# Holding the second-half weights of the output projection behind the first half's, in a one-layer hybrid encoder kernel on Trainium2

## The chip, the cores and the metric

The kernel runs on one core of one Trainium2 chip. A core has a matrix engine (TensorE, "PE" in the profile, with its weight loads shown as "PEld"), a vector engine (VectorE, "DVE"), a scalar engine (ScalarE, "ACT"), a general engine (GpSimd, "POOL") and a queue engine (SyncE, "SP") that mostly asks for transfers between the chip's memory and the core's on-chip memory. Each engine works through its own list of instructions strictly in order; an instruction that waits for another engine or for a transfer holds up all that stands behind it in its list. The metric is the device time of one execution in microseconds (us); the time of a kernel is the median of several executions.

## The reference, cut to what matters

One layer (DEPTH = 1) over 512 tokens of width 1024, with 16 learned tokens put in front and dropped at the end:

```
u      = rmsnorm(h, norm_mix)
proj   = u @ w_in
y_rw   = rwkv7_branch(proj[...])            # 512 columns
y_fx   = fox_branch(proj[...])              # 512 columns
merged = gate_A * (y_rw @ w_out_rw) + gate_B * (y_fx @ w_out_fx)
h      = h + merged @ w_o                   # the output projection
z      = rmsnorm(h, norm_mlp)
h      = h + square(relu(z @ w_up)) @ w_down
```

The change touches the line with `w_o`, a product of 512 x 1024 by 1024 x 1024.

## The kernel before

**Products in three passes.** Every large matrix product is done with operands split in two: a "hi" part, which is the float32 value copied to the matrix engine's shorter float format, and a "lo" part, which is what the copy left out. The product is hi x hi + hi x lo + lo x hi (`passes`, L276), so each tile of weights costs three matmuls, and before that one copy on ACT and one subtraction on DVE. Weights come in chunks of 128 x 512 float32 (256 KB): one transfer on SP's queue into a "raw" tile, then the ACT copy to hi, then the DVE subtraction to lo.

**Two ways of loading a chunk.** `load_h` (L232) takes raw, hi and lo from rings of four tiles each, called wraw, whi and wlo; `load_w` (L242) calls it for two chunks. A new load has to wait until the raw tile of the chunk four before has been read by its subtraction, and a new hi has to wait until the matrix engine has finished with the chunk four before. The list `asked` collects the transfers asked for by `load_h`; it is used later on to order other transfers behind them. `split` (L272) does only the copy and the subtraction (L273 and L274), into whatever tiles it is given.

**The stage around the change.** The work ahead of it merges the two branches: for each of eight column blocks m, two gate tiles gl come in by transfer (L1207), ACT takes their tanh (L1208), the matrix engine makes two products into accumulation banks po (L1213), DVE multiplies each bank by its gate (L1215, which frees the bank), GpSimd adds the two (L1217), ACT writes the hi part mhi (L1218) and DVE the lo part mlo (L1219). After the last mhi one table load on ACT (`pinned`, L265) prepares for later functions. The banks po come from a ring of four.

Then comes the output projection, in two halves of 512 output columns:

- First half (L1236 to L1244): the eight chunks of `wo[0]` come through `load_w`, so through the rings of four. They are called chunk 0 to chunk 7 here. The matrix engine goes through them in this order: for chunks 0 to 5, all four row blocks with one chunk (12 matmuls) before the next chunk; chunks 6 and 7 are taken together, row block by row block. The four sums pd are two po banks and two others; the second po bank is the one that held the second product of merge block m = 6.
- Second half (L1245 to L1248): the eight chunks of `wo[1]` have a place of their own. Their raw tiles are slices of one large tile, shown as zhiraw, which is free at this time, and their hi and lo parts are slices of wohi and wolo. Nothing in a ring holds these loads and splits back.
- After that the first-half sums are added to h (L1254 to L1257), the matrix engine runs the second half (L1274) row block by row block with the transposes (L1264) of the normalised rows between them, and the up-projection follows (L1302), whose first chunks were loaded early (L1234, into zloraw), and whose further chunks come through `load_w` again.

**What sets the order.** In this part of the program nothing fixes the order of the lists by hand. The compile step lays out each engine's list from its own model of times, preferring what is traced first among what it takes to be ready; so a step that is traced later, but is ready sooner in that model, can be placed ahead of an earlier one. The helper `after(ins, prev)` (L251) adds an edge that only orders: `ins` is placed behind `prev`, with no semaphore.

Of the kernel before, what the change touches and what calls it, by code (L numbers as in the profile page):

```python
# [9 lines left out]
F32 = mybir.dt.float32  # L10
# [4 lines left out]
ALU = mybir.AluOpType  # L15
# [172 lines left out]
def kernel(ctx, tc, ht, x, win, par, cst, gain, lora, wout, wo, wup, wdn, out, dbg=None):  # L188
    nc = tc.nc
# [3 lines left out]
    V, G, A = nc.vector, nc.gpsimd, nc.scalar  # L193
# [35 lines left out]

    asked = []  # L230

    def load_h(src, low, tag, bufs):  # L232

        raw = wp.tile([128, 512], F32, name=tag + "raw", bufs=bufs[0])
        asked.append(nc.sync.dma_start(raw, src))
        hi = wp.tile([128, 512], F32R, name=tag + "hi", bufs=bufs[1])
        lo = wp.tile([128, 512], F32R, name=tag + "lo", bufs=bufs[2])
        A.copy(hi, raw)  # L238
        low.tensor_tensor(lo, raw, hi.bitcast(F32), ALU.subtract)  # L239
        return hi, lo  # L240

    def load_w(src, low=(V, V)):  # L242

        return [load_h(src[:, 512 * j:512 * j + 512], low[j], "w", (4, 4, 4)) for j in range(2)]
# [5 lines left out]
    def after(ins, prev):  # L250

        tc.add_manual_dep(ins.ins, prev.ins.name, mybir.DependencyInfo(mybir.DependencyClass.NoSync, mybir.DependencyReason.DATA),
                          reason="one accumulation at a time")
# [16 lines left out]
        return table["pin"]  # L270

    def split(hi, lo, x):  # L272
        A.copy(hi, x)  # L273
        V.tensor_tensor(lo, x, hi.bitcast(F32), ALU.subtract)  # L274

    def passes(w, x):  # L276
        return ((w[0], x[0]), (w[0], x[1]), (w[1], x[0]))
# [8 lines left out]
    with ExitStack() as st:  # L286
# [40 lines left out]
        with tc.tile_pool(name="xp", bufs=2) as xp:  # L327
# [7 lines left out]
            for blk in (B_LORA, B_GD, B_PAIR + 3):  # L335
# [3 lines left out]
                for j in range(2):  # L339
                    raw = wp.tile([128, 512], F32, name="wraw", bufs=4)  # L340
# [57 lines left out]
            with tc.manual_schedule(engines={ET.PE, ET.Activation, ET.DVE, ET.Pool}):  # L398
# [79 lines left out]
                shifts[1](pos[1][1], tks[1])  # L478
            tanh(lf[:64], lf[:64])
            split(lhi[:, B_LORA, :], llo[:, B_LORA, :], lf)  # L480
        y_rw = yp.tile([128, 4, S], F32, name="y_rw")
        y_fx = yp.tile([128, 4, S], F32, name="y_fx")
# [13 lines left out]
        tanh(gf, gf, scale=0.5)  # L496
        V.tensor_scalar(gf, gf, 0.5, 0.5, ALU.mult, ALU.add)
        split(lhi[:, B_GD, :], llo[:, B_GD, :], gf)

        fp = st.enter_context(tc.tile_pool(name="fp", bufs=1))  # L500
# [107 lines left out]
        def divided():  # L608
            yield chained[1]
            for k in range(2):  # L610
                split(*two(0, k), y_rw[:, k, :])
            for k in range(3):
                yield fox_done[k]
                split(*two(1, k), y_fx[:, k, :])
            yield normalised[1][1]
            for k in range(2, 4):
                split(*two(0, k), y_rw[:, k, :])
# [578 lines left out]
    with ExitStack() as st:  # L1196
# [24 lines left out]
        wohi = mp.tile([128, KB, 512], F32R, name="wohi")  # L1221
        wolo = mp.tile([128, KB, 512], F32R, name="wolo")
# [7 lines left out]
        for j in range(2):  # L1230
            we = yp.tile([128, 2, 2, 512], F32R, name=f"we{j}", tag=("y_rw", "y_fx")[j])
            for x in range(2):
                raw = raws[1][:, 2 * j + x, :]
# [5 lines left out]
        for b2 in range(4):  # L1239
            w = load_w(wo[0, b2])  # L1240
            for i, b1 in [(i, b1) for b1 in range(2) for i in range(4)] if b2 < 3 else [(i, b1) for i in range(4) for b1 in range(2)]:
                k = 2 * b2 + b1
                for n, (a, b) in enumerate(passes(M, w[b1])):
                    mm(pd[i], a[:, k, 128 * i:128 * i + 128], b, start=k == 0 and n == 0, stop=k == 7 and n == 2)  # L1244
        for k in range(KB):  # L1245
            raw = raws[0][:, k, :]
            nc.sync.dma_start(raw, wo[1, k // 2][:, 512 * (k % 2):512 * (k % 2) + 512])
            split(wohi[:, k, :], wolo[:, k, :], raw)  # L1248
        zhi = hp.tile([128, KB, S], F32R, name="zhi", tag="zhi")
        zlo = hp.tile([128, KB, S], F32R, name="zlo", tag="zlo")  # L1250
        ssb = mp.tile([128, 4], F32, name="ssb")
# [309 lines left out]
```

## Time and profile before

| | us |
|---|---|
| median of 3 runs | 840.73 (839.65 to 841.92) |
| the profiled execution's own time | 840.95 |
| its span, from first to last instruction | 839.2 |
| PE busy | 826.2 |
| DVE busy | 606.9 |
| ACT busy | 451.9 |
| merge of the branches and output projection, PE | about 395 to 509 of the span |

The granted clock of the matrix engine was 1.000. The profile is of one execution; all times in it count from the first instruction. Lines with "L1244" and the like name a line of the program; a line of a helper (L238, L239, L273, L274) stands for all who call it, so there the tile names tell who it is: whi and wlo from wraw are chunks of the rings, wohi and wolo from zhiraw are the second half. A row of the timeline gives start, duration, engine, line, operation, output and inputs, and how many like it were run together ("x2"); what stands in brackets is the idle time ahead of it and what ended it. Rows of SPq are the asking for a transfer, not the transfer.

### The profile page before, as it was taken

Reading aid. Unit: us, or ns where it says so; the run is one execution under the profiler, and the core shown is the slowest. Engines: PE = TensorE matmul, PEld = TensorE weight load, DVE = VectorE, ACT = ScalarE, POOL = GpSimd, SP = SyncE. Lnnn points to the kernel's source line nnn. Section 1 sums busy time; section 2 is a strip of 40 time slices with the busy share of each in tenths; the row PEclk is TensorE's granted clock in tenths of the full one; section 3 lists DMA queues with packets and bytes.
Section 4 is the critical chain, followed back from the end, with each engine's and each line's share of the span. In section 5 each row is a group of like instructions: output and inputs, shape, how many; then the busy total and the mean of one; then the engine's idle time right before and its main releaser. Section 6 shows DMA issues by size and latency. Waiting matters only on the chain.

```text
span 839.2 us, 15281 instructions
## 1 busy us (share of the span) xinstructions
PE 826.2 (98%) x5758; PEld 679.4 (81%) x5758; DVE 606.9 (72%) x1209; ACT 451.9 (54%) x933; POOL 117.8 (14%) x121
## 2 busy tenths in 40 slices
PE   8999999999999999999999999999999999999998
PEld 6979886686997877687887789888888888888886
DVE  6897976688779665864257644975698569867988
ACT  7767539665754276644357523565445434544452
POOL 1011000001010000000022002100650065007300
PEclk9999999999999999999999999999999999999999
DMA  7231221211112220232588403631753275336531
GB/s 235 73 91 63 65 77 43 65 53 64 54 59 91 89 65 27 76 115 91 186 281 281 140 26 101 201 102 42 255 155 101 74 229 160 90 108 209 160 102 75
DMA packets 51482, 95.88 MB, mean 114 GB/s; under 512 B 5832, under 2 KB 7240, under 8 KB 51408
## 3 DMA queue, kind: packets, MB, share of 16 engines
q1 hardware_dynamic: 47680, 86.38, 32.6%
q0 software_dynamic: 1280, 4.20, 1.7%
q10 hardware_dynamic: 2448, 4.33, 1.5%
q8 instruction: 45, 0.74, 0.4%
q14 instruction: 29, 0.24, 0.1%
HBM read 88.57 MB, written 6.31 MB: 113 GB/s over the span
## 4 chain that ended last, share of the span: by engine, by line
PE 84%; DVE 6%; ACT 4%; DMA 3%; issue 2%; POOL 1%; SPq 0%; DVEq 0%; ACTq 0%; POOLq 0%
PE pj L580 24%; PE po L1302 21%; PE po L1429 12%; PE pd L1429 5%; PE po L1274 3%; PE pw L993 2%; PE psc L738 1%; PE pj L395 1%; DMA gl<-gd 1%; PE py L786 1%; PE ppt L770 1%; PE pch L1059 1%; PE po L1244 1%; PE pd L1244 1%; DVE wlo L550 1%
## 5 line engine op out<-in xcount | busy, mean ns | idle before, releaser
L580 PE MATMUL pj<-uhi,whi 128*128 128x264 f32 (+1 forms) x480 | 164.8, 343 | 0.0
L580 PE MATMUL pj<-ulo,whi 128*128 128x264 f32 (+1 forms) x480 | 154.1, 321 | 0.0
L580 PE MATMUL pj<-uhi,wlo 128*128 128x264 f32 (+1 forms) x480 | 154.0, 321 | 0.0
L239 DVE TENSOR_TENSOR wlo<-wraw,whi 128x512 fp32r<-128x512 f32 x84 | 78.6, 947 | 40.2 <-ACT whi L238 40.0
L580 PEld LDWEIGHTS pj<-uhi,whi 128*128 128x128 f32 x480 | 90.2, 188 | 14.5 <-issue 6.1
L580 PEld LDWEIGHTS pj<-ulo,whi 128*128 128x128 f32 x480 | 90.4, 188 | 7.7 <-issue 2.4
L580 PEld LDWEIGHTS pj<-uhi,wlo 128*128 128x128 f32 x480 | 90.3, 188 | 6.9
L1302 PE MATMUL po<-zhi,whi 128*128 128x512 f32 (+1 forms) x248 | 94.8, 382 | 0.0
L1302 PE MATMUL po<-zlo,whi 128*128 128x512 f32 (+1 forms) x248 | 94.8, 382 | 0.0
L1302 PE MATMUL po<-zhi,wlo 128*128 128x512 f32 (+1 forms) x248 | 94.8, 382 | 0.0
L238 ACT CAST whi<-wraw 128x512 fp32r<-128x512 f32 x84 | 51.5, 618 | 58.7 <-PE po L1302 19.5
L549 ACT CAST whi<-wraw 128x512 fp32r<-128x512 f32 x78 | 47.6, 617 | 43.1 <-PE pj L580 40.7
L550 DVE TENSOR_TENSOR wlo<-wraw,whi 128x512 fp32r<-128x512 f32 x78 | 52.7, 685 | 21.8 <-ACT whi L549 19.2
L273 ACT CAST whi<-t 128x512 fp32r<-128x512 f32 x64 | 39.9, 624 | 44.5 <-DVE wlo L274 27.2
L1429 PE MATMUL po<-wlo,fhi 128*128 128x512 f32 (+1 forms) x164 | 63.4, 387 | 0.1
L1429 PE MATMUL po<-whi,flo 128*128 128x512 f32 (+1 forms) x164 | 62.9, 384 | 0.0
L1429 PE MATMUL po<-whi,fhi 128*128 128x512 f32 (+1 forms) x164 | 62.3, 384 | 0.0
L1351 POOL TENSOR_TENSOR t<-traw 128x512 f32<-128x512 f32 x24 | 37.1, 1561 | 173.5 <-DMA traw<-in_wdn 121.3
L274 DVE TENSOR_TENSOR wlo<-t,whi 128x512 fp32r<-128x512 f32 x64 | 43.6, 689 | 24.3 <-ACT whi L273 24.1
L1318 ACT CAST fhi<-R 128x768 fp32r<-128x768 f32 (+1 forms) x32 | 30.2, 944 | 46.1 <-DVE R L1325 25.1
L1302 PEld LDWEIGHTS po<-zlo,whi 128*128 128x128 f32 x248 | 46.6, 188 | 9.1
L1302 PEld LDWEIGHTS po<-zhi,whi 128*128 128x128 f32 x248 | 46.6, 188 | 9.0
(316 smaller groups left out, 1741.4 us busy)
## 6 DMA issues: line engine op xcount, KB each, us to landing
wraw<-in_win SPq DMA_DIRECT2D x84, 256.0 KB, 2.6
wraw<-in_wup SPq DMA_DIRECT2D x60, 256.0 KB, 3.1
wraw<-in_wdn SPq DMA_DIRECT2D x48, 256.0 KB, 2.7
traw<-in_wdn SPq DMA_DIRECT2D x48, 256.0 KB, 3.6
gd<-gt ACTq DMA_DIRECT2D x16, 256.0 KB, 2.5
wraw<-in_wout SPq DMA_DIRECT2D x16, 256.0 KB, 3.9
gl<-gd SPq DMA_DIRECT2D x16, 256.0 KB, 3.6
traw<-in_wdn POOLq DMA_DIRECT2D x16, 256.0 KB, 3.2
```

Of the source, the lines that this page charges most:

```text
L238: A.copy(hi, raw)
L239: low.tensor_tensor(lo, raw, hi.bitcast(F32), ALU.subtract)
L273: A.copy(hi, x)
L274: V.tensor_tensor(lo, x, hi.bitcast(F32), ALU.subtract)
L549: after(A.copy(hi, raw), last["ACT"])
L550: after(V.tensor_tensor(lo, raw, hi.bitcast(F32), ALU.subtract), last["DVE"])
L580: mm(po, a, b[:, k, a0:a1], start=n == 0, stop=n == 23)
L1274: mm(po, a[:, k, 128 * i:128 * i + 128], b[:, k, :], start=n == 0, stop=n == 23)
L1302: mm(po[:, t0:t1], a, b[:, k, t0:t1], start=n == 0, stop=n == 23)
L1318: A.copy(fhi[:, j, a:b], R[:, a:b])
L1351: eng.tensor_tensor(t, sums[c, pair] if c in (T1, T2) else c, d, ALU.add)
L1429: mm(x[i][:, cols], a[:, k, left, 128 * rows:128 * rows + 128], c[:, cols], start=start and k == 0 and n == 0, stop=stop and k == n_pairs ...
```

## The change

The second half's transfers get an ordering edge: each is placed in SP's list behind `asked[-3]`, which at that point of the program is the transfer of chunk 5 of the first half, the third from the end. The second half's copies and subtractions get edges too: each ACT copy is placed behind the copy of chunk 7, and each DVE subtraction behind the subtraction of chunk 7 (`casts[-1]`). To have these at hand, `load_h` now keeps its two instructions in a list `casts`, and `split` returns its two. No instruction is added, removed or resized, no tile moves, and no semaphore wait is written by hand.

```diff
+    casts = []
+
     def load_h(src, low, tag, bufs):
 
         raw = wp.tile([128, 512], F32, name=tag + "raw", bufs=bufs[0])
         asked.append(nc.sync.dma_start(raw, src))
         hi = wp.tile([128, 512], F32R, name=tag + "hi", bufs=bufs[1])
         lo = wp.tile([128, 512], F32R, name=tag + "lo", bufs=bufs[2])
-        A.copy(hi, raw)
-        low.tensor_tensor(lo, raw, hi.bitcast(F32), ALU.subtract)
+        casts.append((A.copy(hi, raw), low.tensor_tensor(lo, raw, hi.bitcast(F32), ALU.subtract)))
         return hi, lo
...
     def split(hi, lo, x):
-        A.copy(hi, x)
-        V.tensor_tensor(lo, x, hi.bitcast(F32), ALU.subtract)
+        return A.copy(hi, x), V.tensor_tensor(lo, x, hi.bitcast(F32), ALU.subtract)
...
         for k in range(KB):
             raw = raws[0][:, k, :]
-            nc.sync.dma_start(raw, wo[1, k // 2][:, 512 * (k % 2):512 * (k % 2) + 512])
-            split(wohi[:, k, :], wolo[:, k, :], raw)
+            after(nc.sync.dma_start(raw, wo[1, k // 2][:, 512 * (k % 2):512 * (k % 2) + 512]), asked[-3])
+            for x, prev in zip(split(wohi[:, k, :], wolo[:, k, :], raw), casts[-1]):
+                after(x, prev)
```

## The prediction

> **What bounds the kernel now.** I read the page first, then the matrix engine's timeline in the stage of the output projection, then the lists of ACT, DVE and SP over the same stretch, and last the chain of waits.
>
> ```profile
> span 839.2 us, 15281 instructions
> ...
> PE 826.2 (98%) x5758; PEld 679.4 (81%) x5758; DVE 606.9 (72%) x1209; ACT 451.9 (54%) x933; POOL 117.8 (14%) x121
> ...
> PE 84%; DVE 6%; ACT 4%; DMA 3%; issue 2%; POOL 1%; SPq 0%; DVEq 0%; ACTq 0%; POOLq 0%
> ```
>
> The matrix engine bounds the kernel: it is busy for 826.2 of 839.2 us, so moving transfers and splits can pay only where it stands still. Around the change it stands still twice.
>
> ```profile
> 457.03 0.39 PE L1244 MATMUL po<-whi,mhi 128*128 128x512 f32 x1
> ...
> 457.49 0.39 PE L1244 MATMUL po<-whi,mlo 128*128 128x512 f32 x1
> 458.62 0.50 PE L1244 MATMUL po<-whi,mhi 128*128 128x512 f32 x1 [0.75 <-DVE gl L1215]
> ...
> 466.01 0.39 PE L1244 MATMUL pd<-whi,mlo 128*128 128x512 f32 x1
> 466.36 0.50 PE L1244 MATMUL po<-whi,mhi 128*128 128x512 f32 x1
> 467.62 0.50 PE L1244 MATMUL po<-wlo,mhi 128*128 128x512 f32 x1 [0.76 <-DVE wlo L239]
> ...
> 481.13 0.39 PE L1274 MATMUL po<-wohi,mhi 128*128 128x512 f32 x1
> ```
>
> The first half has 96 matmuls (8 chunks, 4 row blocks, 3 passes). The chain of waits gives the pace of an undisturbed run of them:
>
> ```profile
> 481.30 10.88 PE po L1274 x48
> ```
>
> 10.88 / 48 = 0.2267 us each, so 96 take 21.76 us. From the first one (457.03) to the first of the second half (481.13) it took 24.10. Lost: 2.34 us. Stall one: after 457.49 the next was due at 457.72 and came at 458.62, 0.90 late, and that matmul was 0.11 longer. Stall two: 467.62 was due 0.45 after 466.01, so it came 1.16 late, and was again 0.11 longer. That is 2.28 of the 2.34. The 36 matmuls ahead of 466.36 are those of chunks 0 to 2, so stall two is the wait for chunk 3.
>
> **Stall one, part by part.** The engine waits for DVE to empty the bank of merge block 6 (L1215).
>
> ```profile
> 456.57 1.40 DVE L274 TENSOR_TENSOR wolo<-zhiraw,wohi 128x512 fp32r<-128x512 f32 x2 [0.20 <-ACT wohi L273]
> 457.89 0.68 DVE L1215 SCALAR_TENSOR_TENSOR gl<-gl,po 128x512 f32<-128x512 f32 x1
> ```
>
> Two second-half subtractions stand straight ahead of that multiplication; second-half work isn't wanted before 481. With both moved away, the multiplication can start 457.89 - 456.57 = 1.32 us sooner and is over by 457.25, ahead of 457.72. The stall goes, with 0.5 us to spare. (Its gate's tanh is also needed, but was done before 456: the two tanhs in the next fence are those of block 7, the last.)
>
> **Stall two.** ACT's list, and what SP had asked for:
>
> ```profile
> 455.92 1.33 ACT L273 CAST wohi<-zhiraw 128x512 fp32r<-128x512 f32 x2 [1.03 <-DMA zhiraw<-in_wo]
> 457.31 0.63 ACT L1208 ACTIVATE gl<-gl 128x512 f32<-128x512 f32 x1
> ...
> 459.45 0.63 ACT L1208 ACTIVATE gl<-gl 128x512 f32<-128x512 f32 x1 [1.00 <-DMA gl<-gd]
> ...
> 461.08 0.60 ACT L238 CAST whi<-wraw 128x512 fp32r<-128x512 f32 x1
> 462.11 1.27 ACT L273 CAST wohi<-zhiraw 128x512 fp32r<-128x512 f32 x2 [0.42 <-DMA zhiraw<-in_wo]
> 465.16 0.62 ACT L273 CAST wohi<-zhiraw 128x512 fp32r<-128x512 f32 x1 [1.78 <-DMA zhiraw<-in_wo]
> 465.69 0.61 ACT L238 CAST whi<-wraw 128x512 fp32r<-128x512 f32 x1
> 466.21 0.61 ACT L273 CAST wohi<-zhiraw 128x512 fp32r<-128x512 f32 x1
> 466.73 0.62 ACT L1218 ACTIVATE mhi<-gl 128x512 fp32r<-128x512 f32 x1
> 467.37 1.28 ACT L265 ACT_TABLE_LOAD   x1
> 468.67 2.41 ACT L238 CAST whi<-wraw 128x512 fp32r<-128x512 f32 x4
> ```
>
> ```profile
> 454.06 0.38 SPq L235 DMA_DIRECT2D wraw<-in_wo  x1
> ...
> 459.20 0.33 SPq L235 DMA_DIRECT2D wraw<-in_wo  x1
> 459.57 0.91 SPq L1247 DMA_DIRECT2D zhiraw<-in_wo  x2
> 463.21 4.71 SPq L235 DMA_DIRECT2D wraw<-in_wo  x2
> 470.04 13.62 SPq L235 DMA_DIRECT2D wraw<-in_wup  x8
> ```
>
> Counted back from the last two (463.21), the transfer at 459.20 is chunk 5 and the one at 454.06 is chunk 3 (chunk 4's, between them, is left out). The four copies from 468.67 are chunks 4 to 7, so the copy at 465.69 is chunk 3's and the one at 461.08 chunk 2's. From asking to landing, in us, for the second half (the tile's view: least, median, most) and for the first (the view of transfers: median):
>
> ```profile
> L1247 SPq DMA_DIRECT2D zhiraw<-in_wo x8: 422/423/432, 448.7 to 460.0; - x8
> ...
> DMA to landing us min/median/max: 4.4/5.2/5.7
> ```
>
> ```profile
> wraw<-in_wo SPq DMA_DIRECT2D x8, 256.0 KB, 3.8
> ```
>
> Chunk 3, asked for at 454.06, lay on chip by about 460, even with the longest landing seen here (5.7). Its copy came at 465.69, because ACT, in order, stood at second-half copies (462.11 and 465.16) whose transfers, asked for at 459.57, were still on the way: 1.78 us idle in front of the second alone. Those copies will stand behind chunk 7's. In the same order without them, chunk 3's copy follows chunk 2's at about 461.7, and its subtraction (0.69) behind it on DVE is done by about 464, allowing for the gate multiplication between. Deadline: chunk k is wanted at 457.03 + 2.72 k, so chunk 3 at 465.19 and its lo part at 465.42. The stall goes, with over 1 us to spare.
>
> **What is late next: chunk 4.** Wanted at 467.91, its lo part at 468.14. On the old chain it came behind the last mhi and the table load:
>
> ```profile
> 463.09 1.29 DVE L274 TENSOR_TENSOR wolo<-zhiraw,wohi 128x512 fp32r<-128x512 f32 x2
> 464.30 0.68 DVE L1215 SCALAR_TENSOR_TENSOR gl<-gl,po 128x512 f32<-128x512 f32 x1
> ...
> 469.32 2.50 DVE L239 TENSOR_TENSOR wlo<-wraw,whi 128x512 fp32r<-128x512 f32 x4 [0.55 <-ACT whi L238]
> ```
>
> ```profile
> 465.13 1.29 POOL L1217 TENSOR_TENSOR gl<-gl,gl 128x512 f32<-128x512 f32 x1 [4.80 <-DVE gl L1215]
> ```
>
> Chunk 4's lo part was done at about 470.0, so this chain must come 1.9 us sooner. What leaves it: the two subtractions at 463.09 (1.21 to the next start), one more further up of the same kind (0.6), and the copy at 466.21, behind which mhi waited 0.3 after POOL ended at 466.42. That is 2.1 at the least. At the most, DVE and ACT also lose their waits for second-half transfers, another 1.5 or so. So between 0.6 us of new stall (if only 1.3 of this comes) and none; I take none, since 2.1 is the sum of rows that certainly move, and carry 0.6 as a bound.
>
> The table load is the one place where a rule speaks against this. The row has 1.28 us, and the next copy starts at 468.67, 0.02 behind it. The Trainium skill, page "ScalarE: Activation LUTs", section "What ACT_TABLE_LOAD costs", gives 1.28 us plus 1.38 of draining; by that chunk 4 would be 1.36 later and the gain about 1.1 instead of 2.3 (an estimate by that page). The trace shows no such drain on either side of this load (mhi ends at 467.35, the load starts at 467.37), so the sum keeps 1.28.
>
> **Chunks 5 to 7** are wanted at 470.63, 473.35 and 474.03. Chunk 5's place in the ring comes free when the engine is done with chunk 1 (462.5), 6's at 465.2, 7's at 467.9, and copy plus subtraction are 1.3 us; no stall if they have landed (rival two).
>
> **The second half itself** is wanted from 478.79 (457.03 + 21.76), chunk k 0.68 k later. Its splits can't start before chunk 7's, at 467.9 at the soonest, and at about 472 if chunk 7 lands late. Eight subtractions at 0.61 to 0.69 us are 5.5 us, so they end between 474 and 478 while the first is wanted at 478.79 and the last at 483.5. That work moves from 453 to 467, where DVE and ACT were short, to a stretch where both idle:
>
> ```profile
> 456.80:468.70 11.90, 10.39 (x44) 7.77 (x43) 9.54 (x15) 8.58 (x15) 2.90 (x2) 1.00 0.59 204
> 468.70:481.30 12.60, 12.60 (x57) 10.45 (x56) 6.14 (x12) 5.56 (x12) 0.00 (x0) 1.00 0.46 144
> ```
>
> The columns are stretch, length, busy PE, PEld, DVE, ACT, POOL, clock, DMA share, GB/s. After the move DVE has some 11.6 of 12.6 us in the second stretch (6.14 + 5.5): full, but with 5 us to its deadline. The up-projection's transfers (470.04) are paced by the ring and wanted only after the second half. Sum: -2.3 us of stalls, +0 new. Against the profiled execution's 840.95 that is 838.65; the median of runs is 0.22 lower, so 838.4.
>
> **Rivals.** *One: a shorter stall stays, at chunk 4 or at the bank.* The margins above are 0.2 to 0.5 us, and the compile step may set the released work in another order. New stalls of 0.6 to 1.3 leave a gain of 1.0 to 1.7: 839.0 to 839.7, say 839.4. Against it: all three places lose work, none gains any. Its largest form is a table load that holds ACT another 1.3 us after its row (839.6); with the next copy 0.02 behind the row I give that 0.01 of this rival's chance.
>
> *Two: chunk 6 comes late.* SP may place all eight second-half transfers between chunks 5 and 6, in 8 x 0.42 = 3.4 us of asking. If transfers on one queue are served in the order asked, chunk 6's follows 2.1 MB. At 204 GB/s (the first window above) nine transfers take 11.6 us; asked for from 459.57 they end at 471.2, and with the 1.3 of the split chunk 6 is ready at 472.5, inside 473.35. It stalls only if chunk 5 is asked for more than 0.9 later than it was; with 2 us later, 1.1 is lost: gain 1.2, 839.5. The Trainium skill, page "DMA: Bandwidth & Descriptors", section on queues, rings and completion order, says that each transfer engine consumes a ring's descriptors in the order of the ring, which is this rival's premise; the longer landing of zhiraw (5.2 against 3.8) fits it. Against it: chunk 5 is asked for when chunk 1's subtraction is done, and that gets earlier.
>
> *Three: nothing moves.* Other early work, such as the splits of early up-projection chunks, takes the freed places and the two stalls stay: 840.7. Against it: the rows in front of both stalls are second-half rows, by name.
>
> *Four, slower: the second half comes too late.* The edge puts no upper limit on how far back SP places these transfers. If they land behind the eight up-projection transfers, they are asked for from 483.66 (470.04 + 13.62). With the 3.8 of the first half's transfers the first lands at 487.5, its split takes 1.3, and the second half starts at 488.8 instead of 478.8: 10.0 lost against 2.3 won, 848.4. It decides from about 476, from where on the first would be ready after 481.13. Against it: second-half transfers are traced first and have free tiles the moment chunk 5 is asked for.
>
> **How the numbers follow.** Forecast 0.64, rival one 0.19, two 0.06, three 0.06, four (with any disorder further on) 0.05. What a measurement of this kernel can tell from no change is about 0.3%, 2.5 us, so faster means under 838.2. The forecast lies at 0.28%, just inside; the three runs of before span 2.3 us (839.65 to 841.92), and the forecast's own range is 837.6 to 839.0 (chunk 4's bound of 0.6 above, scatter below). So 0.3 faster (a little under half of the forecast), 0.65 within (the rest of it and rivals one to three), 0.05 slower. The range 837.4 to 840.0 holds the forecast and rivals one and two and leaves out three and four and some scatter.
>
> **What would show it.** Right: no idle time of the matrix engine between 457 and 479, the first L1274 matmul at 478.8 to 479.2, wohi copies in one block behind chunk 7's copy at 468 to 473, and no wait of ACT for zhiraw. Step one is wrong if 458.62 still waits for L1215; step two if chunk 3's copy comes after 464.5; the chunk 4 bound is met if a wait for wlo shows near 468. The whole is wrong if the stretch from 457 to 481 shrinks by 2.3 and the span doesn't, for then the time was given back further on, or if SP asks for zhiraw behind in_wup.

## The result, and the profile after

| | before | after |
|---|---|---|
| median of 12 runs each, us | 841.25 (839.65 to 842.45) | 838.62 (838.01 to 839.82) |
| ratio, 95% interval | | 0.9974 (0.9966 to 0.9982) |
| the profiled execution, us | 840.95 | 838.08 |
| its span, us | 839.2 | 836.3 |

The changed kernel is 0.26% faster, 2.2 us by the ratio and 2.6 by the medians. The prediction was 838.4 with a range of 837.4 to 840.0. Below, "the pass" is the whole piece that the change can reach: from the first matmul of the first half to the last of the second.

**Where the time went.** Busy time of the engines by stretch, first before and then after: the first half, and all behind it. The columns are those of the windows in the prediction. (Some lines of the changed program are numbered one or two higher: the copies and subtractions of `load_h` are both L240, those of `split` both L274, the second half's matmuls L1275. L1207 to L1247 keep their numbers.)

```profile
457.03:481.13 24.10, 22.59 (x97) 17.86 (x96) 15.46 (x26) 13.74 (x25) 2.90 (x2) 1.00 0.52 174
481.13:839.20 358.07, 354.15 (x1653) 295.81 (x1651) 265.88 (x366) 164.10 (x274) 84.99 (x64) 1.00 0.41 128
```

```profile
456.53:478.29 21.76, 21.76 (x98) 18.02 (x96) 15.72 (x26) 13.63 (x26) 2.65 (x2) 1.00 0.66 223
478.29:836.30 358.01, 354.11 (x1653) 295.80 (x1651) 266.08 (x366) 163.89 (x274) 84.87 (x64) 1.00 0.41 128
```

The first row of each carries the result: 24.10 us became 21.76, which is 96 matmuls at the undisturbed pace and no more, and its busy time equals its length. The second differs by 0.06, so nothing was given back. The first half also began 0.50 sooner (456.53 against 457.03). By the timeline 0.20 of that was there at 423 us already, and the rest came between 424 and 425, where two matmuls of the merge came late in before; no instruction that the change touches stands there yet, so I count the 0.50 as a difference between two executions, not as a gain.

**The two places of the stalls.** The timeline of ACT after, then DVE and SP:

```profile
458.74 1.13 ACT L240 CAST whi<-wraw 128x512 fp32r<-128x512 f32 x2
463.14 0.63 ACT L1218 ACTIVATE mhi<-gl 128x512 fp32r<-128x512 f32 x1 [3.27 <-POOL gl L1217]
463.79 1.28 ACT L266 ACT_TABLE_LOAD   x1
465.08 1.67 ACT L240 CAST whi<-wraw 128x512 fp32r<-128x512 f32 x3
468.50 0.62 ACT L240 CAST whi<-wraw 128x512 fp32r<-128x512 f32 x1 [1.75 <-DMA wraw<-in_wo]
469.03 4.27 ACT L274 CAST wohi<-zhiraw 128x512 fp32r<-128x512 f32 x8
```

```profile
455.45 0.68 DVE L1215 SCALAR_TENSOR_TENSOR gl<-gl,po 128x512 f32<-128x512 f32 x1
...
461.27 0.68 DVE L240 TENSOR_TENSOR wlo<-wraw,whi 128x512 fp32r<-128x512 f32 x1
...
465.74 1.90 DVE L240 TENSOR_TENSOR wlo<-wraw,whi 128x512 fp32r<-128x512 f32 x3 [1.24 <-ACT whi L240]
...
469.77 4.90 DVE L274 TENSOR_TENSOR wolo<-zhiraw,wohi 128x512 fp32r<-128x512 f32 x8
```

```profile
458.53 1.38 SPq L1247 DMA_DIRECT2D zhiraw<-in_wo  x3
...
462.16 0.38 SPq L237 DMA_DIRECT2D wraw<-in_wo  x1
462.58 1.60 SPq L1247 DMA_DIRECT2D zhiraw<-in_wo  x3
466.45 14.36 SPq L237 DMA_DIRECT2D wraw<-in_wup  x8
```

DVE empties the bank of block 6 from 455.45 to 456.13 (before: from 457.89), 1.1 us ahead of its need at 457.21, the fourth matmul. Chunks 2 and 3 are copied in one row at 458.74, chunk 3 therefore near 459.3 (before: 465.69), with the subtraction at 461.27. All eight second-half copies stand in one block behind chunk 7's, at 469.03. In these rows ACT is idle only for GpSimd ahead of the last mhi and for chunk 7's own transfer, where before it stood at second-half transfers (further up, ahead of 458.74, it still waits for gate transfers).

### The profile page after: what moved, and what is told of

It reads as the page before. It is cut to its first block, busy times and chain, and to the rows that moved or that the text cites. A ratio compares the mean times of both kernels' runs of the same rounds, so it can differ in the third digit from the quotient of the medians.

```text
span 836.3 us, 15281 instructions
## 1 busy us (share of the span) xinstructions
PE 824.9 (99%) x5758; PEld 679.5 (81%) x5758; DVE 606.8 (73%) x1209; ACT 450.4 (54%) x933; POOL 117.5 (14%) x121
## 4 chain that ended last, share of the span: by engine, by line
PE 90%; DVE 5%; ACT 3%; issue 1%; DVEq 0%
PE pj L580 24%; PE po L1303 21%; PE po L1430 12%; PE po L1213 5%; PE pd L1430 5%; PE po L1275 3%; PE pw L993 2%; PE pj L395 1%; PE psc L738 1%; PE pd L1244 1%; PE po L1244 1%; PE py L786 1%; PE ppt L770 1%; PE pch L1059 1%; DVE wlo L550 1%
## 5 line engine op out<-in xcount | busy, mean ns | idle before, releaser
L240 DVE TENSOR_TENSOR wlo<-wraw,whi 128x512 fp32r<-128x512 f32 x84 | 78.8, 949 | 39.0 <-ACT whi L240 39.0
L240 ACT CAST whi<-wraw 128x512 fp32r<-128x512 f32 x84 | 51.2, 617 | 54.9 <-PE po L1303 17.6
L274 ACT CAST whi<-t 128x512 fp32r<-128x512 f32 x64 | 39.9, 624 | 44.4 <-DVE wlo L274 27.2
L274 DVE TENSOR_TENSOR wlo<-t,whi 128x512 fp32r<-128x512 f32 x64 | 43.6, 690 | 24.3 <-ACT whi L274 24.0
L1303 PEld LDWEIGHTS po<-zhi,wlo 128*128 128x128 f32 x248 | 46.6, 188 | 9.0
```

What stands on the lines that cost most here:

```text
L240: casts.append((A.copy(hi, raw), low.tensor_tensor(lo, raw, hi.bitcast(F32), ALU.subtract)))
L274: return A.copy(hi, x), V.tensor_tensor(lo, x, hi.bitcast(F32), ALU.subtract)
L1303: mm(po[:, t0:t1], a, b[:, k, t0:t1], start=n == 0, stop=n == 23)
```

## The experiments

The theories. **A, the lists**: first-half steps stood on ACT and DVE behind second-half steps that waited for transfers or took their turn; what counts is the order of those two lists. **B, the transfers**: the second half's traffic delayed the first half's, and moving the requests is what pays. **D, the place**: the gain hangs on the requests' place behind chunk 5. Two theories, **E and F**, came up on the way and concern the matrix engine's clock: E, it falls only after a long stretch with little matrix work; F, a stop of 1.5 us is enough.

Ratios are against the kernel before, timed beside each kernel; "first half" runs from its first matmul to the first of the second half, "the pass" to the start of the last matmul of the second half.

| kernel | us (runs) | ratio, 95% interval | first half, us | pass, us |
|---|---|---|---|---|
| before, first profile | 841.25 (12) | | 24.10 | 47.44 |
| before, second profile | 843.26 (1) | | 26.62 | 49.96 |
| after | 838.62 (12) | 0.9974 (0.9966 to 0.9982) | 21.76 | 45.09 |
| splits only | 838.87 (11) | 0.9970 (0.9958 to 0.9981) | 21.76 | 45.09 |
| requests only | 840.19 (11) | 0.9988 (0.9975 to 1.0001) | 23.55 | 46.88 |
| requests only, again | 841.74 (1) | | 24.58 | 47.91 |
| requests, and DVE's edge | 838.66 (1) | | 22.09 | 45.42 |
| splits of the last five | 839.22 (11) | 0.9974 (0.9962 to 0.9986) | 22.00 | 45.34 |
| splits of the first three | 840.78 (11) | 1.0000 (0.9983 to 1.0017) | 26.22 | 49.55 |
| requests behind chunk 7 | 838.37 (10) | 0.9974 (0.9964 to 0.9983) | 21.76 | 45.10 |
| splits behind row block 1 | 838.23 (7) | 0.9963 (0.9949 to 0.9976) | 22.01 | 45.50 |
| splits behind row block 2 | 840.10 (10) | 0.9985 (0.9975 to 0.9994) | 23.41 | 46.89 |
| splits behind row block 3 | 843.39 (8) | 1.0029 (1.0018 to 1.0039) | 24.92 | 50.01 |

### Splits only: the requests stay free

```diff
-            after(nc.sync.dma_start(raw, wo[1, k // 2][...]), asked[-3])
+            nc.sync.dma_start(raw, wo[1, k // 2][...])
```

> Only the splits are held behind chunk 7's; the second half's transfers have no edge, and SP's list is that of before, while the lists of ACT and DVE are those of the changed kernel. Theory A (the order of the ACT and DVE lists made both stalls): the first half takes 21.8 us, at most 22.1 (chunk 4 has little to spare if gate transfers land as late as before), and the time is 2.0 to 2.4 us under before, within 0.3 us of the changed kernel. Theory B (the second half's transfers delayed the gates and the first-half chunks): both stalls stay for the most part, 23 to 24.1 us, less than 1.1 us gained.

SP asks in the order of the kernel before, second-half requests between those of the first half (two rows of its timeline), while ACT's and DVE's lists are those of after:

```profile
455.41 0.33 SPq L237 DMA_DIRECT2D wraw<-in_wo  x1
455.79 0.90 SPq L1247 DMA_DIRECT2D zhiraw<-in_wo  x2
```

The first half takes 21.76, the time is that of after within the intervals. The whole gain is there without moving a request, so B falls as the cause of it.

### Requests only: the splits stay free

```diff
-            for x, prev in zip(split(wohi[:, k, :], wolo[:, k, :], raw), casts[-1]):
-                after(x, prev)
+            split(wohi[:, k, :], wolo[:, k, :], raw)
```

> Only the transfers are held behind chunk 5's; the splits are free, and the compiled ACT list has one second-half copy ahead of a first-half one, two ahead of the table load, three ahead of chunk 5 and two ahead of chunk 6, all of transfers asked for later than before. Theory A: ACT waits for zhiraw again, 2 to 5 us in all, and the matrix engine stands still for 0.2 to 1.5 us of new places (chunks 3 to 5), so the gain is 0.8 to 2.1 us, less than that of holding the splits. Theory B: the whole gain, 2.3 us, first half 21.8 us.

> The kernel with only the transfers held, once more. Its ACT list puts second-half copies ahead of first-half ones, so its stall (1.8 us in the first profile, at chunk 4) is there again, 0.3 to 2 us, after a wait of ACT for zhiraw; without such a wait, none.

Some two fifths of the gain are left in the timed runs (ratio 0.9988, with no change just inside the interval). ACT now meets the second-half copies even earlier relative to their transfers. Its timeline, and then the matrix engine's, in the first of the two profiles:

```profile
462.44 0.62 ACT L274 CAST wohi<-zhiraw 128x512 fp32r<-128x512 f32 x1 [3.08 <-DMA zhiraw<-in_wo]
462.96 0.62 ACT L240 CAST whi<-wraw 128x512 fp32r<-128x512 f32 x1
...
466.17 0.63 ACT L1218 ACTIVATE mhi<-gl 128x512 fp32r<-128x512 f32 x1 [1.49 <-POOL gl L1217]
...
468.11 0.62 ACT L240 CAST whi<-wraw 128x512 fp32r<-128x512 f32 x1
```

```profile
468.78 0.50 PE L1244 MATMUL po<-whi,mhi 128*128 128x512 f32 x1 [0.93 <-ACT whi L240]
469.51 0.50 PE L1244 MATMUL po<-wlo,mhi 128*128 128x512 f32 x1 [0.22 <-DVE wlo L240]
```

Chunk 3 gets through, chunk 4 is late: its copy starts at 468.11, where 465.08 is the row of after, and it was due at 467.67 (456.79 + 4 x 2.72). This is the place that the prediction called "late next". The second profile of the same program lost more, 24.58, with stalls at chunk 3 and at chunk 4: the size of the loss belongs to the execution. Both losses, 1.79 and 2.82 over the floor of 21.76, are larger than expected (0.2 to 1.5, then 0.3 to 2).

### Requests, and the edge of DVE alone

```diff
-            for x, prev in zip(split(wohi[:, k, :], wolo[:, k, :], raw), casts[-1]):
-                after(x, prev)
+            after(split(wohi[:, k, :], wolo[:, k, :], raw)[1], casts[-1][1])
```

> Transfers held as in the change, the subtractions held on DVE, the copies on ACT free; DVE's list is that of the changed kernel, ACT's is that of the kernel in which only the transfers were held. Theory A, with ACT as the list that matters: a first half like in that kernel, longer than 21.8 us by whatever ACT's waits for zhiraw cost there. If DVE is the list that matters: 21.8 us.

ACT's list is that of requests only; DVE's is that of after. DVE's timeline, first requests only, then this kernel:

```profile
463.09 0.69 DVE L274 TENSOR_TENSOR wolo<-zhiraw,wohi 128x512 fp32r<-128x512 f32 x1 [2.32 <-ACT wohi L274]
463.70 0.68 DVE L1215 SCALAR_TENSOR_TENSOR gl<-gl,po 128x512 f32<-128x512 f32 x1
```

```profile
460.96 0.68 DVE L1215 SCALAR_TENSOR_TENSOR gl<-gl,po 128x512 f32<-128x512 f32 x1
```

ACT still waits for second-half transfers here (2.20, 0.24 and 1.02 us by its rows), yet only 0.33 us of the first half is lost. The difference is the last gate multiplication: at 463.70 behind a subtraction that waited for ACT's late copy, at 460.96 without it. GpSimd's addition, the last mhi, the table load and chunk 4 hang on it. So a wait on ACT reached the matrix engine mostly by way of DVE's list; the 22.09 lies close to the 21.8 of the expectation's second case. ACT's order alone still cost the 0.33: it falls at chunk 5, whose copy (469.41) stood behind the second-half copy that waited 1.02. DVE's order alone, with the copies held on ACT, was not run, and these are single profiles.

### Splits of the last five, and of the first three

```diff
-            after(nc.sync.dma_start(raw, wo[1, k // 2][...]), asked[-3])
+            nc.sync.dma_start(raw, wo[1, k // 2][...])
...
-                after(x, prev)
+                if k >= 3:
+                    after(x, prev)
```

The other kernel has `k < 3`.

> No edge on transfers; the splits of second-half chunks 3 to 7 are held, those of 0 to 2 are free and stand where they stood before. Theory A: stall one (0.9 to 1.0 us, the bank behind two subtractions) stays and stall two goes: first half 22.7 to 22.9 us, gain 1.2 to 1.4 us. Theory B: transfers as before, so both stalls stay, about 24.1 us.

> The other way round: the splits of second-half chunks 0 to 2 are held, those of 3 to 7 free. Theory A: stall one goes and stall two (chunk 3 behind copies that wait for their transfers, 1.2 to 1.4 us) stays: first half 22.9 to 23.2 us, gain 0.9 to 1.2 us. Theory B: both stay, about 24.1 us.

With the last five held, 22.00: only 0.24 is lost, not the 0.9 to 1.0 of stall one. DVE's timeline shows the two subtractions still straight ahead of the gate multiplication, but earlier. First comes the row of before that stands ahead of its two subtractions (456.57) and its multiplication (457.89), then this kernel:

```profile
455.68 0.69 DVE L239 TENSOR_TENSOR wlo<-wraw,whi 128x512 fp32r<-128x512 f32 x1
```

```profile
455.21 0.68 DVE L240 TENSOR_TENSOR wlo<-wraw,whi 128x512 fp32r<-128x512 f32 x1
455.81 1.28 DVE L274 TENSOR_TENSOR wolo<-zhiraw,wohi 128x512 fp32r<-128x512 f32 x2
457.02 0.68 DVE L1215 SCALAR_TENSOR_TENSOR gl<-gl,po 128x512 f32<-128x512 f32 x1
```

The multiplication starts 0.05 us behind the first matmul at 456.97; in the profile of before it started 0.86 behind it (457.89 against 457.03). Half of the difference of 0.81 was there before DVE came to the two subtractions: the row ahead of them starts 1.76 us before the first matmul here and 1.35 in before, 0.41 later. The other 0.40 is ACT's wait of 1.03 us for the transfers of its two copies, of which DVE felt only this much (0.20 of idle time, the rest in slower turns); here the copies didn't wait. So the two subtractions' turn, 1.2 to 1.3 us, made a stall of 0.24 where DVE came to them in time, and of 0.90 where it came late. With the first three held, stall one is gone and stall two is there, larger than expected, and then the clock falls. The profiled execution took 843.07 us, against the median of 840.78: its clock fell, as in one more of the 11, so the 26.22 of the table is more than the usual execution loses. The timeline of the matrix engine:

```profile
465.33 0.39 PE L1244 MATMUL pd<-whi,mlo 128*128 128x512 f32 x1
466.23 0.50 PE L1244 MATMUL po<-whi,mhi 128*128 128x512 f32 x1 [0.51 <-ACT whi L240]
468.11 0.61 PE L1244 MATMUL po<-wlo,mhi 128*128 128x512 f32 x1 [1.38 <-DVE wlo L240]
```

In time this kernel can't be told from before. What mattered most are the five splits whose transfers were asked for last.

### Requests behind chunk 7

```diff
-            after(nc.sync.dma_start(raw, ...), asked[-3])
+            after(nc.sync.dma_start(raw, ...), asked[-1])
```

> The changed kernel with the transfers held behind that of chunk 7 instead of chunk 5, so that all eight are asked for after the whole first half (from about 462.6). The lists of ACT and DVE are those of the changed kernel. Theory A: the last lands by about 472.5, its split is done by 474, still over 4 us ahead of the first need at 478.3: first half 21.8 us, time within 0.3 us of the changed kernel. Theory D (the place of the transfers was fitted, and either side of it loses): over 0.5 us slower than the changed kernel.

The time is the same and the first half again 21.76, so D falls. One row of ACT differs:

```profile
467.93 0.62 ACT L240 CAST whi<-wraw 128x512 fp32r<-128x512 f32 x1 [1.19 <-PE pd L1244]
```

Chunk 7's copy waits for its place in the ring, not, as after, 1.75 us for its transfer. So second-half transfers asked for ahead of chunk 7 did delay it after, to 468.50. That is 11.97 us after the first matmul, against 11.08 here (467.93 - 456.85): a delay of 0.9, since the rest of the 1.75 would have gone to waiting for the ring. Chunk 7 was due only at 473.53 (456.53 + 6.25 x 2.72), so this cost nothing.

### Splits held too far back

The splits are traced behind the sums and squares of the first half and held behind those of row block 1, 2 or 3 (here 2):

```diff
+        for k in range(KB):
+            for x, prev in zip(split(wohi[:, k, :], wolo[:, k, :], raws[0][:, k, :]), (squares_[2], sums_[2])):
+                after(x, prev)
```

> The changed kernel, but each second-half split is held behind the last square (ACT) and the last sum (DVE) of the first half instead of chunk 7's split. In the changed kernel these ended at 480.5 and 479.8, while the second half wanted its first split at 478.3. Theory A (a deadline counted from the matrix engine's pace): first hi at about 481.1, first lo at 481.8, so the second half starts 2.9 us late and loses another 0.4 at its first lo: 3.3 us over the changed kernel, 1.0 over before. Theory C (the second half has slack that the deadline does not see, since the engine can go on with other work): within 0.5 us of the changed kernel.

> The second-half splits are held behind the square and the sum of row block 1 of the first half instead of block 3. By the lists and durations of the kernel that was too late, the first hi is done 21.3 us after the first half's start (wanted at 21.8) and the first lo at 22.0 (wanted at 22.0), so the first pair is just in time; the third pair stands behind the square of block 2 and its lo comes 0.8 to 0.9 late, the sixth behind that of block 3 some 0.3. Theory A (deadlines from the pace): 0.8 to 1.3 us over the changed kernel, still 1.0 to 1.5 under before, clock 1.0 throughout. Theory C (no price before the first pair is late): the time of the changed kernel.

> The same behind block 2. First hi at 23.4 after the start (1.6 late), first lo 0.5 later still, the third pair another 0.4: 2.1 to 2.6 us over the changed kernel, so within 0.4 us of before, if the matrix engine's clock holds. Theory E (the clock falls only after about 3 us with next to no matmul, as in the two kernels where it fell): clock 1.0. Theory F (1.5 us are enough): matmuls at half pace for about 3.5 us after the stall, another 1.6 us, so 1.2 to 1.9 us over before.

This is the mechanism of the rival on the slower side, made small. The matrix engine's timeline for row block 2 and for row block 3:

```profile
477.83 0.39 PE L1244 MATMUL pd<-whi,mlo 128*128 128x512 f32 x1
479.71 1.20 PE L1276 MATMUL po<-wohi,mhi 128*128 128x512 f32 x4 [1.49 <-ACT wohi L274]
```

```profile
478.87 0.39 PE L1244 MATMUL pd<-whi,mlo 128*128 128x512 f32 x1
482.26 1.76 PE L1275 MATMUL po<-wohi,mhi 128*128 128x512 f32 x4 [3.00 <-ACT wohi L274]
483.82 0.63 PE L1275 MATMUL po<-wolo,mhi 128*128 128x512 f32 x1
```

Row block 3 stops the engine for 3.16 us (482.26 - 478.87 - 0.23), and the pass is 4.92 longer than after's: nearly all of the other 1.76 is the clock, since matmuls then come 0.43 apart instead of 0.23 until 485.96. That brings the kernel to 843.39, 2.4 over before, where 1.0 was expected: the clock was not in that sum. Row block 2 stops it for 1.65, and the pass is 1.80 longer at an unbroken clock of 1.00. Row block 1 was expected to cost about 1 and cost 0.4 in the pass and nothing in time: with the splits late, the compile step put two hi x hi matmuls in a row at 480.53 (four at the start in the other two kernels, the "x4" above), so the engine could work before the next subtraction was done. That changed order also took some of row block 2's loss, 1.80 where 2.1 to 2.6 was expected. The prediction's deadline holds: the first hi part was done 1.62 us late with row block 2 and 3.13 with row block 3 (copies at 479.06 and 481.61, 0.62 long), and the engine stopped for 1.65 and 3.16, until in the second case the clock joined in.

### The kernel before, once more

> The kernel before, once more, for a second profile. If the two stalls are a fixed property of the lists, they are 0.9 and 1.2 us again (first half 24.1). If they hang on when single transfers land, each moves by some tenths to a microsecond: first half 22.5 to 25 us, with the wait of ACT for zhiraw moving with stall two.

The same program, 26.62 us instead of 24.10 for its first half, more than the 22.5 to 25 expected, and the stalls are elsewhere. The timelines of the matrix engine, of GpSimd and of ACT:

```profile
457.95 0.50 PE L1244 MATMUL po<-whi,mhi 128*128 128x512 f32 x1 [0.47 <-DVE gl L1215]
...
470.14 0.50 PE L1244 MATMUL po<-whi,mhi 128*128 128x512 f32 x1 [1.55 <-ACT whi L238]
470.86 0.50 PE L1244 MATMUL po<-wlo,mhi 128*128 128x512 f32 x1 [0.22 <-DVE wlo L239]
...
471.94 0.63 PE L1244 MATMUL po<-whi,mlo 128*128 128x512 f32 x1
```

```profile
464.68 2.81 POOL L1217 TENSOR_TENSOR gl<-gl,gl 128x512 f32<-128x512 f32 x1 [5.34 <-DVE gl L1215]
```

```profile
463.74 0.62 ACT L273 CAST wohi<-zhiraw 128x512 fp32r<-128x512 f32 x1 [0.89 <-DMA zhiraw<-in_wo]
464.27 0.61 ACT L238 CAST whi<-wraw 128x512 fp32r<-128x512 f32 x1
...
467.52 0.63 ACT L1218 ACTIVATE mhi<-gl 128x512 fp32r<-128x512 f32 x1 [2.12 <-POOL gl L1217]
```

Stall one is 0.62 long instead of 0.90, chunk 3 comes in time (464.27 instead of 465.69, its transfers landed sooner), and the engine waits 1.55 for chunk 4, because GpSimd's last addition took 2.81 us instead of the 1.29 of the first profile, while DVE ran one subtraction after another. Then the clock falls as well. What the kernel before has is a list without slack from 457 to 470; where it breaks differs from one execution to the next.

## Why the prediction was right, point by point

- **The bound and the sum.** The size was right to the second digit: 2.34 us to be had, and the first half came down by 2.34, to the floor of 96 x 0.2267. The term is right for the profiled execution and only for that: the second profile of before would have given 4.86. That one profile gave nearly the timed difference, 2.6 by the medians and 2.2 by the ratio, is in part luck: its time, 840.95, lay near the median of before, 841.25, and the second profile's, 843.26, did not. What the prediction took for the least visible change, 0.3%, was too coarse: 12 runs of each gave an interval of 0.16%.
- **Stall one.** Gone, with 1.1 us to spare where 0.5 was reckoned. The two subtractions named there were the last link, and taking their 1.32 us away was enough. That they cost 0.90 in that execution hung on more: DVE came to them 0.41 late, and another 0.40 was ACT's wait for transfers handed on. The run with only the last five held kept the two subtractions without this lateness and lost 0.24, so that step of the prediction was right in effect and too narrow in cause, and so was the expectation for that run.
- **Stall two.** Gone as worked out: chunk 3's subtraction was done by 461.95 (461.27 + 0.68), earlier than the "about 464" of the text.
- **Chunk 4, the bound of 0.6.** Not needed. Its lo part was done at about 466.43 (465.74 + 0.69), 9.90 after the first matmul; before it was 12.97. That is 3.07 sooner, between the 2.1 "at the least" and the 3.6 "at the most". The worry was real, though: with only the requests moved, or in the second profile of before, chunk 4 is where the engine stops.
- **The table load.** It takes 1.28 us and the next copy starts 0.01 behind its end (463.79 + 1.28 = 465.07, 465.08). The Trainium skill, page "ScalarE: Activation LUTs", section "What ACT_TABLE_LOAD costs", adds 1.38 of draining; no drain shows at this load, here or in any run.
- **The second half.** Wanted at 478.29 (0.5 ahead of the predicted 478.8 to 479.2, since the first half began 0.50 sooner), first split done by 470.46 (469.77 + 0.69), the last by 474.67. "474 to 478" was on the safe side: chunk 7 came at 468.50, not 472.
- **Rival one** (a shorter stall elsewhere) did not come in after, but is just what the requests alone give. **Rival two** had its premise in part: three second-half requests stood ahead of chunk 6 and five ahead of chunk 7, whose copy came 0.9 us later for it, with about 4 us to spare. **Three** is excluded by the lists. **Four**: SP placed every second-half request ahead of the up-projection's (462.58 against 466.45); the late row blocks show what its mechanism costs, and a part of the price that it left out, the clock.
- **Not foreseen**: that the stalls of before differ between executions by over 2 us, and that a long one costs twice, once as the stop and once as the slower clock after it.

No version here beats after by more than the intervals allow, and the first half has nothing left to give. The split edges alone do the same work as the whole change.

## What to carry to other kernels

On an engine that works in order, a step for later that waits for its transfer is paid by whatever stands behind it, and the lists of two engines hand such waits on to each other; so hold late work behind the early work's last step on every engine that takes both, and ask first whether its deadline leaves room. Moving the requests without the steps that wait for them can lengthen the wait. Size a stall from its floor (what the bound engine needs undisturbed) and not from one profile's waits, since the waits of a tight list move from execution to execution.

## What the runs showed of the hardware that was not expected

**The granted clock falls after a long stall.** Windows of 2 us, for the kernel with the first three splits held and then for the second profile of before:

```profile
466.00:468.00 2.00, 0.50 (x1) 0.19 (x1) 2.00 (x3) 1.16 (x3) 1.51 (x1) 1.00 0.00 0
468.00:470.00 2.00, 1.89 (x5) 1.50 (x6) 1.26 (x3) 1.97 (x3) 0.00 (x0) 0.59 0.35 113
470.00:472.00 2.00, 2.00 (x7) 1.59 (x6) 1.86 (x3) 1.14 (x3) 0.00 (x0) 0.56 0.10 35
472.00:474.00 2.00, 2.00 (x11) 1.60 (x10) 0.84 (x3) 1.47 (x3) 0.00 (x0) 1.00 0.87 291
```

```profile
472.00:474.00 2.00, 2.00 (x6) 1.59 (x5) 0.61 (x2) 0.00 (x0) 0.00 (x0) 0.50 0.90 291
474.00:476.00 2.00, 2.00 (x7) 1.56 (x6) 0.18 (x1) 0.62 (x1) 0.00 (x0) 0.69 0.65 227
```

The clock column reads 0.50 where the low stretch fills the window. By shorter windows that stretch lasts from 468.36 to 471.77 and from 471.83 to 475.24, and from 482.64 to 486.06 with the splits behind row block 3: 3.41 to 3.42 us each time, with matmuls 0.43 us apart, and then 1.00 again. 1.6 to 1.7 us are lost each time. Counted from start to start of matmuls, it fell after 2.78 us with one in between (465.33 to 468.11), after 3.39 us with none (row block 3), and behind 2.66 us with one in between (468.20 to 470.86) when matmuls had been running again for 1.1 us. It didn't fall after 1.88 us with none (row block 2, where all ten executions kept a mean clock of 0.999 or more), nor after 2.05 us with one in between (requests only, 467.46 to 469.51). That speaks against F, and the falls after 2.78 and 2.66 us come a little sooner than the 3 us of E. The Trainium skill, page "TensorE: Matmul & The Clock Gate", section "Part 1: The HAM clock gate", says that the clock halves after an idle window of about 3.4 us which runs freely, and recovers after as long of work: recovery agrees with these rows, and the late fall at 471.94 suits a window that doesn't start with the stall, but each fall came with some matmul time inside the last 3.4 us.

How little work counts as idle can be narrowed by an estimate: in the 3.41 us ahead of each fall the matrix engine was busy for 1.52 (first three), 1.64 (second profile of before) and 0.41 us (row block 3), and in the emptiest 3.41 us of this stage in profiles without a fall for 1.92 (row block 2), 2.25 and 2.28 (requests only, twice) and 2.65 (before). If it is the busy time in such a stretch that counts, the limit lies between 1.64 and 1.92 us, about half; that the chip looks back this far is not shown.

In the timed runs the mean clock was 0.998 or less in 5 of 66 executions of before (843.4 to 845.6 us), in 6 of 8 with the splits behind row block 3, and in none of 33 of after, splits only and requests behind chunk 7. That fits a pass without stops, but 33 executions are few: at a rate of 5 in 66 they would show none about one time in thirteen (an estimate). The difference of medians hardly holds any of it: without the five, the medians of before in their sets move by 0.1 us at most, and none of the 12 executions of before in the result's table reached 843.

**GpSimd's addition and DVE's subtractions wait for each other.** The addition of L1217, the same work each time, took 1.29 us, 1.61 and 2.81 by its rows. One of them in the profile of after, with the subtraction beside it:

```profile
456.28 1.29 POOL L1217 TENSOR_TENSOR gl<-gl,gl 128x512 f32<-128x512 f32 x1 [3.33 <-ACT gl L1208]
```

```profile
456.81 1.31 DVE L240 TENSOR_TENSOR wlo<-wraw,whi 128x512 fp32r<-128x512 f32 x1 [0.67 <-ACT whi L240]
```

A subtraction on DVE, 0.69 us elsewhere, took 1.31 after (at 456.81, with the addition running from 456.28) and 1.76 with the first three held (at 466.30, with the addition from 465.89 to 467.51). The prediction's margins counted 0.69 throughout; the last one made stall two of that run 1.1 longer. The rows look like taking turns rather than like running slower together. A subtraction that starts during an addition ends 0.55 us behind the addition's end (457.57 and 458.12 here, 467.51 and 468.06 there), and an addition that starts during a subtraction ends 1.15 us behind it (466.34, the end of DVE's third step in a row, and 467.49 in the second profile of before). In the 13 profiles nearly all such pairs of the merge keep these two distances to 0.03. A gate multiplication, which reads one input from an accumulation bank, did not hold the addition up: at 424.33 after, with the multiplication running, it took 1.29. What the two engines share, no run here took apart.
